# Steps of three late chains at set places between weight matmuls, GLA's odd queries side by side, and a bank of their own for the last columns

## The chip, the cores and the metric

The kernel runs on one core of one Trainium2 chip. The metric is device time in microseconds (us); a comparison takes the median of several runs. TensorE (PE) multiplies, VectorE (DVE) and ScalarE (ACT) do elementwise work and reductions, GpSimd (POOL) is hardly used, SyncE (SP) issues the transfers. PEld is TensorE's loading of stationary weights.

## The reference

One decoder layer on x of 256 tokens by 2048, all in float32:

```python
h = rms_norm(x, norm1_gain) * (1 + scale1) + shift1          # scale, shift, gate: silu(c) @ w_ada + b_ada
proj = h @ w_in                                              # 13840 columns, split among three branches
o_sb  = stick-breaking attention, 6 heads, q and k normalised
o_dil = 3 groups of 2 heads, windows (128, 1), (512, 4), (2048, 16), ALiBi, mixed by softmax of their log-denominators
o_gla = gated linear attention, 4 heads of 128 x 256, rms_norm, times silu(r)
y = g0 * (o_sb @ w_br_sb) + g1 * (o_dil @ w_br_dil) + g2 * (o_gla @ w_br_gla)      # g: sigmoid of gate columns
x = x + gate1 * (y @ w_out)
h = rms_norm(x, norm2_gain) * (1 + scale2) + shift2
x = x + gate2 * ((silu(h @ w_gate) * (h @ w_up)) @ w_ffn_out)
```

## The kernel before, in words

**Weight matmuls.** A weight block is 512 columns wide. `load_weights` (L125) brings two 128-row pieces at a time through four `raw` buffers, ScalarE rounds them to `whi` (L148) and VectorE subtracts (L149, "split") to get `wlo`. Activations are kept transposed, as a high and a low part too. `mm3` (L153) adds three products per 128-row piece k and per half t of the 256 tokens, each with 512 moving columns. `block` (L158) runs k over a block's rows, both halves inside.

**Order.** The kernel is written in a tile framework: the program is traced in order, and a builder then fixes each engine's instruction order by priority and by its own idea of when an operand is ready; on the chip each engine keeps that order. `prio()` lifts what is traced inside it ahead by 4000 places. `tc.issue_after(ins)` keeps an instruction behind another on the same engine. `tick` runs background work (the sums of `silu(c) @ w_ada` for the later modulations, on VectorE) at a set rate beside the blocks. Transposes and attention use four "misc" PSUM banks, weight blocks four "acc" banks. Scratch tiles ("scr") have three buffers.

**First chunks' h.** `first_group` (L475) forms the modulation of the first three 128-row chunks. After the last multiply-add of 16 over the conditioning (`last_mac`, L510), chunk 0's sum over partitions is a matmul with a column of ones (L301); chunks 1 and 2 are transposed (L526) and reduced by VectorE (L529), each reduction behind the low part of the chunk before. `finish_columns` (L312) adds bias and gain, `make_h` (L412) gives ScalarE's high part (L417) and VectorE's low part (L424).

**GLA.** Within a 128-token half, scores are built by levels L = 1, 2, 4, ..., 64 (`gla`, L747): keys of even segments of length L against queries of odd ones. `scatter` (L735) multiplies, for each half and each of four heads, the first 128 - L columns against the last 128 - L, and a masked copy (L742) writes what belongs to the level. A float32 matmul stands twice in the trace, since it is done in two records.

**Dilated attention.** `dilated` (L797) turns q and k (L621), computes scores (L807, L808) and their exponentials for six heads. `mixture` (L834) scales the rows of one head (L849), transposes them (L854), copies them to SBUF on ScalarE (L856) and multiplies by v (L857, L858), head by head. `dilated` is called after the first of two blocks of GLA's output gate (L941), `mixture` between the second and the third block of the branch gates (L962).

**Norm 2.** The last block of `w_out` is done half by half (L1112), and so is the first FFN block (L1141). After each half of `w_out`, `residual` (L1066) adds to x and `norm2` (L1075) forms the scale from the sum of squares (`rsqrt`, L237), and for each of four 512-column pieces scales (L1082), transposes (L1085), applies gain and shift (L1089), and splits (L1093, L1094).

**The end.** The last block of `w_ffn_out` is done half by half from row piece 30 on (L1192). `add_out` (L1172) multiplies by gate 2, adds x and stores; for the last half in two pieces of 256 columns.

Of the kernel before, what the change touches and what calls it, by code (L numbers as in the profile page):

```python
# [17 lines left out]
P = 128  # L18
# [21 lines left out]
NFF = 11  # L40
RANK = 16
# [25 lines left out]
def trunk(ctx: ExitStack, tc: tile.TileContext, I, out):  # L67
# [90 lines left out]
    def block(pss, act, src, k0, k1, c0, base=0, w=None, tiles=range(NT), go_on=False, more=False, seeded=False):  # L158
# [70 lines left out]
    def turn_vectors():  # L229
# [5 lines left out]
        nc.scalar.copy(bada, bada_ps)  # L235

# [203 lines left out]
    def proj_block(g, b, w=None, carry=False):  # L440
# [10 lines left out]
        block(pss, h_at, w_in, k0, k1, b * NB, w=w, go_on=go_on, more=carry, seeded=seeded)  # L451
# [23 lines left out]
    def first_group():  # L475
# [191 lines left out]
    def gla():  # L667
# [59 lines left out]
        sc_same = [S(f"T{2 + t}", [P, N_GLA, P]) for t in range(NT)]  # L727
        nc.vector.memset(sc_same[0], 0.0)
        nc.vector.memset(sc_same[1], 0.0)
# [5 lines left out]
        def scatter(level, lhs, rhs, L=0):  # L735

            n = P - L
            for t in range(NT):
                ps = misc_bank([P, N_GLA, P])
                for h in range(N_GLA):  # L740
                    nc.tensor.matmul(ps[:n, h, L:], at(lhs, h, t)[:, :n], at(rhs, h, t)[:, L:], start=True, stop=True)  # L741
                nc.vector.copy_predicated(  # L742
                    sc_same[t][:n, :, L:], lvl[:n, level : level + 1, L:].to_broadcast([n, N_GLA, n]), ps[:n, :, L:]
                )

        scatter(len(GLA_LEVELS), kT, qT)
        for li, L in enumerate(GLA_LEVELS + (P,)):  # L747
# [7 lines left out]
            if L < P:  # L755
                scatter(li, f, f, L)
# [17 lines left out]
        for t in range(NT):  # L774
            o = S(f"A{9 + t}", [P, N_GLA, T])
            for h2 in range(2):
                ps = misc_bank([P, 2, T])
                ss = small([P, 2])
                for i in range(2):
# [3 lines left out]
                    nc.tensor.matmul(ps[:, i, :], sc_same[t][:, h, :], vh(h, t), start=t == 0, stop=True)  # L783
# [13 lines left out]
    def dilated():  # L797
        qk_turn(dil_parts, state["mm"].ins)
# [4 lines left out]
        for h in range(N_DIL):  # L803
            cq, ck = 18 + h, 24 + h
            slope = 2.0 ** (-8.0 * (h + 1) / N_DIL)
            z = misc_bank([P, W3])
            nc.tensor.matmul(z[:, 0:P], head(cq, 0), head(ck, 0), start=True, stop=True)  # L807
            nc.tensor.matmul(z[:, P:W3].rearrange("p (t d) -> p t d", t=NT), head(cq, 1), head2(ck), start=True, stop=True)  # L808
            lg = prob[h // 2][:, h % 2, :]
            nc.vector.scalar_tensor_tensor(lg, dist[:, h // 2, :], -slope, z, op0=ALU.mult, op1=ALU.add)  # L810
            nmx = small([P, NT])
            for t, (a, b) in enumerate(spans):
                nc.vector.reduce_max(mx[:, t, h : h + 1], lg[:, a:b], axis=AX.X)
                nc.vector.tensor_scalar(nmx[:, t : t + 1], mx[:, t, h : h + 1], -1.0, None, op0=ALU.mult)
                nc.scalar.activation(
                    lg[:, a:b], lg[:, a:b], AF.Exp, bias=nmx[:, t : t + 1], accum_out=sm[:, t, h : h + 1]
                )

        lse = small([P, NT, N_DIL])
        nc.scalar.activation(lse, sm, AF.Ln)  # L820
        nc.vector.tensor_add(lse, lse, mx)
        G = lambda x, g: x[:, :, 2 * g : 2 * g + 2]
        m2 = small([P, NT, 2])
        nc.vector.tensor_max(m2, G(lse, 0), G(lse, 1))
        nc.vector.tensor_max(m2, m2, G(lse, 2))
        for g in range(3):
            nc.vector.tensor_tensor(G(lse, g), G(lse, g), m2, op=ALU.subtract)
        nc.scalar.activation(lse, lse, AF.Exp)
        den = small([P, NT, 2])
        nc.vector.tensor_add(den, G(lse, 0), G(lse, 1))  # L830
        nc.vector.tensor_add(den, den, G(lse, 2))
        return prob, sm, lse, den, spans

    def mixture(prob, sm, lse, den, spans):  # L834
# [5 lines left out]
        nc.vector.tensor_mul(coef, coef, lse)  # L840
        oT = S("OD", [P, 2, 2, T], F32R)
        for j in range(2):
            o = misc_bank([P, T])
            for g in range(3):
                h = 2 * g + j
                cv = 30 + h
                p = prob[g][:, j, :]
                for t, (a, b) in enumerate(spans):
                    nc.vector.tensor_scalar(p[:, a:b], p[:, a:b], coef[:, t, h : h + 1], None, op0=ALU.mult)  # L849

                pt = misc_bank([P, W3])
                for i in range(3):
                    with tc.issue_after(state["mm"].ins):
                        nc.tensor.transpose(pt[:, i * P : (i + 1) * P], p[:, i * P : (i + 1) * P], ident)  # L854
                pT = scr([P, W3])
                nc.scalar.copy(pT, pt)  # L856
                nc.tensor.matmul(o, head(cv, 0), pT[:, 0:T], start=g == 0, stop=False)  # L857
                nc.tensor.matmul(o[:, P:T], head(cv, 1), pT[:, T:W3], start=False, stop=g == 2)  # L858
            split_from_psum(oT[:, 0, j, :], oT[:, 1, j, :], o)
        return oT  # L860
# [69 lines left out]

    rr = []
# [298 lines left out]
```

## Time and profile before

| | us |
|---|---|
| median of 3 runs | 1616.99 (1616.95 to 1617.47) |
| profiled execution | 1617.29 |
| its span, first to last instruction | 1615.5 |
| TensorE busy | 1601.9 |
| VectorE busy | 1119.4 |
| ScalarE busy | 795.2 |
| bytes read from HBM | 392.53 MB |

The profile is of one execution; its span is a little shorter than its device time, which holds what lies before the first and after the last instruction. A timeline row reads: start, length, engine, line, operation, out<-in, partitions x elements, and how many like it were merged; in brackets the idle time of the engine before it and what ended it. A group's row gives busy time, mean ns of one, idle time before. Windows give busy time and count of each engine in a stretch, then granted clock, DMA share and GB/s. A matmul's recorded length is longer than the distance to the next one, since matmuls overlap in the array.

### The profile page before, as it was taken

Reading aid. Unit: us, or ns where it says so; the run is one execution under the profiler, and the core shown is the slowest. Engines: PE = TensorE matmul, PEld = TensorE weight load, DVE = VectorE, ACT = ScalarE, POOL = GpSimd, SP = SyncE. Lnnn points to the kernel's source line nnn. Section 1 sums busy time; section 2 is a strip of 40 time slices with the busy share of each in tenths; the row PEclk is TensorE's granted clock in tenths of the full one; section 3 lists DMA queues with packets and bytes.
Section 4 is the critical chain, followed back from the end, with each engine's and each line's share of the span. In section 5 each row is a group of like instructions: output and inputs, shape, how many; then the busy total and the mean of one; then the engine's idle time right before and its main releaser. Section 6 shows DMA issues by size and latency. Waiting matters only on the chain.

```text
span 1615.5 us, 19941 instructions
## 1 busy us (share of the span) xinstructions
PE 1601.9 (99%) x7336; PEld 1322.0 (82%) x7336; DVE 1119.4 (69%) x1301; ACT 795.2 (49%) x1116; POOL 5.3 (0%) x14
## 2 busy tenths in 40 slices
PE   8999999999999999999999999999999999999998
PEld 7888888788878888888887888888888888888887
DVE  6899995869888787878657566667645555455453
ACT  5654458765865434444446544444444444433332
POOL 1000000000000000000000000000000000000000
PEclk9999999999999999999999999999999999999999
DMA  9999997865868889898666578888666666666663
GB/s 337 355 332 323 333 301 246 268 209 171 286 209 264 305 300 312 299 313 299 229 193 199 161 250 258 267 268 272 199 187 187 189 185 191 189 205 197 205 208 106
DMA packets 194593, 395.94 MB, mean 245 GB/s; under 512 B 12914, under 2 KB 27928, under 8 KB 194496
## 3 DMA queue, kind: packets, MB, share of 16 engines
q1 hardware_dynamic: 194096, 394.60, 75.1%
q8 instruction: 57, 0.93, 0.2%
q14 instruction: 40, 0.33, 0.1%
q10 hardware_dynamic: 176, 0.07, 0.0%
q0 software_dynamic: 224, 0.01, 0.0%
HBM read 392.53 MB, written 2.10 MB: 244 GB/s over the span
## 4 chain that ended last, share of the span: by engine, by line
PE 91%; DMA 3%; DVE 3%; ACT 2%; issue 1%; SPq 0%; DVEq 0%; ACTq 0%
PE acc L156 28%; PE acc L155 28%; PE acc L154 28%; DVE wlo L149 1%; PE misc L741 1%; PE misc L1016 1%; PE acc L405 1%; DMA raw<-w_in 1%; ACT whi L148 1%; DMA raw<-w_br_gla 0%; DMA A<-x 0%; PE misc L398 0%; DVE T L259 0%; DMA T<-w_ada 0%; DMA OS<-w_ada 0%
## 5 line engine op out<-in xcount | busy, mean ns | idle before, releaser
L149 DVE TENSOR_TENSOR wlo<-raw,whi 128x1024 fp32r<-128x1024 f32 (+1 forms) x546 | 652.1, 1199 | 439.3 <-ACT whi L148 437.6
L148 ACT CAST whi<-raw 128x1024 fp32r<-128x1024 f32 (+1 forms) x546 | 562.6, 1032 | 704.9 <-PE acc L156 578.7
L154 PE MATMUL acc<-whi,H 128*128 128x512 f32 x1576 | 616.4, 391 | 1.1 <-ACT H L417 1.0
L156 PE MATMUL acc<-whi,H 128*128 128x512 f32 x1576 | 615.5, 391 | 0.4 <-DVE H L424 0.4
L155 PE MATMUL acc<-wlo,H 128*128 128x512 f32 x1576 | 615.5, 391 | 0.1
L156 PEld LDWEIGHTS acc<-whi,H 128*128 128x128 f32 x1576 | 295.8, 188 | 62.9 <-DVE H L424 1.6
L154 PEld LDWEIGHTS acc<-whi,H 128*128 128x128 f32 x1576 | 296.0, 188 | 62.2 <-ACT H L417 1.9
L155 PEld LDWEIGHTS acc<-wlo,H 128*128 128x128 f32 x1576 | 296.0, 188 | 60.5 <-DVE wlo L149 0.8
L155 PE MATMUL acc<-wlo,A 128*128 128x512 f32 x312 | 121.5, 390 | 0.5 <-DVE wlo L149 0.5
L154 PE MATMUL acc<-whi,A 128*128 128x512 f32 x312 | 121.9, 391 | 0.0
L156 PE MATMUL acc<-whi,A 128*128 128x512 f32 x280 | 109.0, 389 | 0.0
L259 DVE SCALAR_TENSOR_TENSOR ada<-AR,csil,ada 128x1024 f32<-128x1024 f32 x59 | 75.2, 1278 | 1.3 <-DMA AR<-w_ada 1.3
L155 PEld LDWEIGHTS acc<-wlo,A 128*128 128x128 f32 x312 | 58.6, 188 | 12.8 <-DVE wlo L149 0.9
L154 PEld LDWEIGHTS acc<-whi,A 128*128 128x128 f32 x312 | 58.6, 188 | 12.1
L156 PEld LDWEIGHTS acc<-whi,A 128*128 128x128 f32 x280 | 52.6, 188 | 10.9
L154 PE MATMUL acc<-whi,T 128*128 128x512 f32 x120 | 46.7, 389 | 0.0
L155 PE MATMUL acc<-wlo,T 128*128 128x512 f32 x120 | 46.7, 389 | 0.0
L156 PE MATMUL acc<-whi,T 128*128 128x512 f32 x120 | 46.7, 389 | 0.0
L156 PE MATMUL acc<-whi,OS 128*128 128x512 f32 x112 | 43.6, 389 | 0.0
L461 ACT COPY A<-acc 128x512 f32<-128x512 f32 x50 | 29.2, 586 | 18.4 <-PE acc L156 17.2
L259 DVE SCALAR_TENSOR_TENSOR ada<-OS,csil,ada 128x1024 f32<-128x1024 f32 (+2 forms) x33 | 35.6, 1077 | 1.2 <-DMA OS<-w_ada 1.0
L463 DVE TENSOR_TENSOR A<-A,acc 128x512 f32<-128x512 f32 x48 | 31.5, 682 | 2.1 <-PE acc L156 1.8
(337 smaller groups left out, 1212.3 us busy)
## 6 DMA issues: line engine op xcount, KB each, us to landing
raw<-w_in SPq DMA_DIRECT2D x205, 512.0 KB, 4.9
raw<-w_ffn_in SPq DMA_DIRECT2D x176, 512.0 KB, 3.8
raw<-w_ffn_out SPq DMA_DIRECT2D x88, 512.0 KB, 4.5
AR<-w_ada SPq DMA_DIRECT2D x79, 512.0 KB, 4.9
raw<-w_out SPq DMA_DIRECT2D x32, 512.0 KB, 4.0
KC<-w_ada SPq DMA_DIRECT2D x30, 512.0 KB, 5.7
OS<-w_ada SPq DMA_DIRECT2D x16, 512.0 KB, 6.5
raw<-w_br_gla SPq DMA_DIRECT2D x16, 512.0 KB, 6.4
```

Source lines behind the costliest of these rows:

```text
L148: state["cast"] = nc.scalar.copy(hi[:, :n, :], raw[:, :n, :])
L149: state["split"] = nc.vector.tensor_tensor(lo[:, :n, :], raw[:, :n, :], hi[:, :n, :].bitcast(F32), op=ALU.subtract)
L154: nc.tensor.matmul(ps, lh, rh, start=start, stop=False, skip_group_check=seeded)
L155: nc.tensor.matmul(ps, lh, rl, start=False, stop=False, skip_group_check=seeded)
L156: state["mm"] = nc.tensor.matmul(ps, ll, rh, start=False, stop=stop, skip_group_check=seeded)
L259: nc.vector.scalar_tensor_tensor(acc, raw, c, acc, op0=ALU.mult, op1=ALU.add)
L405: state["warm"] = nc.tensor.matmul(ps, ones_r, wide, start=True, stop=True)
L461: nc.scalar.copy(A[b][:, t, :], pss[t])
L463: nc.vector.tensor_add(A[b][:, t, :], A[b][:, t, :], pss[t])
L741: nc.tensor.matmul(ps[:n, h, L:], at(lhs, h, t)[:, :n], at(rhs, h, t)[:, L:], start=True, stop=True)
L1016: nc.tensor.transpose(ps[:, i, :], src[:, i * P : (i + 1) * P], ident)
```

## The change

Five edits. (1) In `first_group` all three last multiply-adds come first, and chunk 1 is summed by the matmul with ones, as chunk 0. (2) In GLA, a level's matmuls move only the queries of odd segments, 64 columns, side by side, for both halves into one bank, and one masked copy writes all. The zeroed score tile of both halves is one tile. (3) Dilated attention is cut into steps that `block` calls ahead of row piece k, behind the matmul before it and with priority: two turns and two score steps in the second block of GLA's output gate, and, after all rows have been scaled, turns and products in the second block of the branch gates. (4) Norm 2 scales all four pieces into one 2048-column tile right after its half; its 16 transposes and what follows are a step at k = 10 of the other half and k = 11 of the first FFN block's first half. The scale is applied as two factors, and two small multiplies fall away. (5) In the last half, the last four row pieces are multiplied for the first 256 columns, then for the last 256 into another bank; the first 256 columns and the part sums of the last are added to x while those run.

```diff
+N2_AT = (10, 11)
...
 def block(..., steps=None):
+            if steps and k - k0 in steps:
+                with tc.issue_after(state["mm"].ins), prio():
+                    steps[k - k0]()
...
+    def rsqrt_parts(ss, inv_n, shape):
+        v = small(shape)
+        nc.vector.tensor_scalar(v, ss, inv_n, EPS, op0=ALU.mult, op1=ALU.add)
+        y = small(shape)
+        nc.scalar.activation(y, v, AF.Ln)
+        nc.scalar.activation(y, y, AF.Exp, scale=-0.5)
+        z = small(shape)
+        nc.vector.scalar_tensor_tensor(z, y, y, v, op0=ALU.mult, op1=ALU.mult)
+        nc.vector.tensor_scalar(z, z, -0.5, 1.5, op0=ALU.mult, op1=ALU.add)
+        return y, z
...
-        last_mac(0)
-        last_mac(1)
+        for q in range(n):
+            last_mac(q)
...
-            if q == 0:
+            if q < 2:
                 sums = misc_bank([P, 2])
...
-            if q == 0:
-                with tc.issue_after(state["finish"].ins):
-                    last_mac(2)
...
-        def scatter(level, lhs, rhs, L=0):
-            n = P - L
-            for t in range(NT):
-                ps = misc_bank([P, N_GLA, P])
-                for h in range(N_GLA):
-                    nc.tensor.matmul(ps[:n, h, L:], at(lhs, h, t)[:, :n], at(rhs, h, t)[:, L:], start=True, stop=True)
-                nc.vector.copy_predicated(
-                    sc_same[t][:n, :, L:], lvl[:n, level : level + 1, L:].to_broadcast([n, N_GLA, n]), ps[:n, :, L:]
-                )
+        def scatter(level, f, L):
+            n, ns = P - L, P // (2 * L)
+            odd = lambda x: x.rearrange("p (s two l) -> p s two l", two=2, l=L)[:, :, 1, :]
+            ps = misc_bank([P, NT * N_GLA, P // 2])
+            for t in range(NT):
+                for h in range(N_GLA):
+                    nc.tensor.matmul(
+                        ps[:n, t * N_GLA + h, :].rearrange("p (s l) -> p s l", l=L), at(f, h, t)[:, :n], odd(at(f, h, t)),
+                        start=True, stop=True,
+                    )
+            dst = sc_same.rearrange("p b (s two l) -> p b s two l", two=2, l=L)[:n, :, :, 1, :]
+            mask = lvl[:n, level, :].rearrange("p (s two l) -> p s two l", two=2, l=L)[:, :, 1, :]
+            nc.vector.copy_predicated(
+                dst, mask.unsqueeze(1).to_broadcast([n, NT * N_GLA, ns, L]),
+                ps[:n].rearrange("p b (s l) -> p b s l", l=L)
+            )
...
+    def mixture_rows(prob, sm, lse, den, spans):
...
+        for h in range(N_DIL):
+            p = prob[h // 2][:, h % 2, :]
+            for t, (a, b) in enumerate(spans):
+                nc.vector.tensor_scalar(p[:, a:b], p[:, a:b], coef[:, t, h : h + 1], None, op0=ALU.mult)
+    def mixture(prob):
+        oT = S("OD", [P, 2, 2, T], F32R)
+        def turn(j):
+            out = []
+            for g in range(3):
+                pt = misc_bank([P, W3])
+                for i in range(3):
+                    nc.tensor.transpose(pt[:, i * P : (i + 1) * P], prob[g][:, j, i * P : (i + 1) * P], ident)
+                pT = scr([P, W3])
+                nc.scalar.copy(pT, pt)
+                out.append(pT)
+            return out
...
+        def first():
+            turned.append(turn(0))
+        def second():
+            products(0, turned[0])
+            turned.append(turn(1))
+        return oT, {4: first, 7: second, 10: lambda: products(1, turned[1])}
...
+    dil_scores, dil_weights = dilated()
+    dil_steps = {
+        2: lambda: qk_turn(dil_parts[:2]),
+        5: lambda: qk_turn(dil_parts[2:]),
+        8: lambda: dil_scores(0, 3),
+        11: lambda: dil_scores(3, 6),
+    }
...
-        block(pss, h_at, w_in, 0, KC, (13 + j) * NB)
+        block(pss, h_at, w_in, 0, KC, (13 + j) * NB, steps=dil_steps if j else None)
...
-        if j == 0:
-            groups = dilated()
...
-    for br in range(2):
-        gate_block(0, br)
+    with prio():
+        groups = dil_weights()
+        mixture_rows(*groups)
+    gate_block(0, 0)
     ring["tags"] = ("AR0", "AR1", "KC", "KD")
-    od = mixture(*groups)
+    od, turns = mixture(groups[0])
+    gate_block(0, 1, turns)
     gate_block(0, 2)
...
-    def norm2(t):
+    def norm2_rows(t):
...
+        r, r2 = rsqrt_parts(ss, 1.0 / D, [P, 1])
+        xs = S("ada", [P, D])
+        for j in range(KC // 4):
+            nc.vector.tensor_scalar(
+                xs[:, j * NB : (j + 1) * NB], x2[j][:, t, :], r, r2, op0=ALU.mult, op1=ALU.mult
+            )
+        return xs
+    def norm2_turn(t, xs):
...
         for j in range(KC // 4):
-            xs = scr([P, NB])
-            nc.vector.tensor_scalar(xs, x2[j][:, t, :], r, None, op0=ALU.mult)
             ps = misc_bank([P, 4, P])
             for i in range(4):
-                nc.tensor.transpose(ps[:, i, :], xs[:, i * P : (i + 1) * P], ident)
+                k = 4 * j + i
+                nc.tensor.transpose(ps[:, i, :], xs[:, k * P : (k + 1) * P], ident)
+            banks.append(ps)
+        for j, ps in enumerate(banks):
...
-        block({t: ps}, y_at, None, 0, KC, 0, w=w, tiles=(t,))
+        block({t: ps}, y_at, None, 0, KC, 0, w=w, tiles=(t,), steps={N2_AT[0]: lambda: norm2_turn(0, xs)} if t else None)
         with prio():
             residual(3, t, ps)
-            norm2(t)
+            xs = norm2_rows(t)
...
-                block(pg, h2_at, None, 0, KC, 0, w=w, tiles=(t,))
+                block(pg, h2_at, None, 0, KC, 0, w=w, tiles=(t,), steps=None if t else {N2_AT[1]: lambda: norm2_turn(1, xs)})
...
+            block(pss, act_at, None, CUT, KF - LASTK, 0, w=w, tiles=(1,), go_on=True, more=True)
+            side = acc_bank()
+            for cols, ps in ((slice(0, NB - LASTC), pss[1][:, : NB - LASTC]), (slice(NB - LASTC, NB), side[:, :LASTC])):
+                for k in range(KF - LASTK, KF):
+                    wh, wl = w[k - CUT]
+                    h, l = act_at(k, 1)
+                    mm3(ps, h, l, wh[:, cols], wl[:, cols], k == KF - LASTK and cols.start > 0, k == KF - 1)
+                if cols.start == 0:
+                    add_out(n, 1, pss[1], end=NB - LASTC)
+                    add_out(n, 1, pss[1], NB - LASTC, store=False)
+            add_out(n, 1, side, NB - LASTC, base=NB - LASTC)
```

More of the change, by code (lines that the diff above doesn't have):

```diff
@@ L156, in mm3, with block @@
         state["mm"] = nc.tensor.matmul(ps, ll, rh, start=False, stop=stop, skip_group_check=seeded)
-    def block(pss, act, src, k0, k1, c0, base=0, w=None, tiles=range(NT), go_on=False, more=False, seeded=False):
+    def block(pss, act, src, k0, k1, c0, base=0, w=None, tiles=range(NT), go_on=False, more=False, seeded=False,
+              steps=None):
         if w is None:
@@ L450, in proj_block @@
             go_on = True
-        block(pss, h_at, w_in, k0, k1, b * NB, w=w, go_on=go_on, more=carry, seeded=seeded)
+        block(pss, h_at, w_in, k0, k1, b * NB, w=w, go_on=go_on, more=carry, seeded=seeded, steps=steps)
         if carry:
@@ L802, in dilated @@
         spans = ((0, P), (P, W3))
[L803 to L816, printed above, removed]
-                )
@@ L830, in dilated, with scores @@
[L830 to L834, printed above, removed]
+        def scores(h0, h1):
+            for h in range(h0, h1):
+                cq, ck = 18 + h, 24 + h
+                slope = 2.0 ** (-8.0 * (h + 1) / N_DIL)
+                z = misc_bank([P, W3])
+                nc.tensor.matmul(z[:, 0:P], head(cq, 0), head(ck, 0), start=True, stop=True)
+                nc.tensor.matmul(z[:, P:W3].rearrange("p (t d) -> p t d", t=NT), head(cq, 1), head2(ck), start=True, stop=True)
+                lg = prob[h // 2][:, h % 2, :]
+                nc.vector.scalar_tensor_tensor(lg, dist[:, h // 2, :], -slope, z, op0=ALU.mult, op1=ALU.add)
+                nmx = small([P, NT])
+                for t, (a, b) in enumerate(spans):
+                    nc.vector.reduce_max(mx[:, t, h : h + 1], lg[:, a:b], axis=AX.X)
+                nc.vector.tensor_scalar(nmx, mx[:, :, h], -1.0, None, op0=ALU.mult)
+                for t, (a, b) in enumerate(spans):
+                    nc.scalar.activation(
+                        lg[:, a:b], lg[:, a:b], AF.Exp, bias=nmx[:, t : t + 1], accum_out=sm[:, t, h : h + 1]
+                    )
@@ L835, in mixture @@
+        return scores, weights
+    def mixture_rows(prob, sm, lse, den, spans):
         G = lambda x, g: x[:, :, 2 * g : 2 * g + 2]
```

89 lines of the change are left out of this document (45 added, 44 removed).

## The prediction

> **What bounds the kernel now.** I read the page first (busy shares and the chain), then TensorE's busy time in a stretch that holds nothing but weight matmuls, then TensorE's waits by releaser, then the timeline of the five places that the change touches.
>
> ```profile
> PE 1601.9 (99%) x7336; PEld 1322.0 (82%) x7336; DVE 1119.4 (69%) x1301; ACT 795.2 (49%) x1116; POOL 5.3 (0%) x14
> ...
> PE 91%; DMA 3%; DVE 3%; ACT 2%; issue 1%; SPq 0%; DVEq 0%; ACTq 0%
> ...
> L154 PE MATMUL acc<-whi,H 128*128 128x512 f32 x1576 | 616.4, 391 | 1.1 <-ACT H L417 1.0
> ```
>
> TensorE is busy 99% of the span, and 91% of the chain that ended last is TensorE. A matmul's recorded length (391 ns) is modelled, so I ask how far apart matmuls start. In a stretch of the down projection without any other TensorE work:
>
> ```profile
> 1400.00:1590.00 190.00, 190.00 (x840) 1.00 0.64 202
> ```
>
> 840 matmuls of 512 columns in 190.0 us are 0.226 us each, at clock 1.00. The change takes away no weight matmul. So it can win only what TensorE stands still, or a cheaper small matmul. TensorE's waits that the profile names:
>
> ```profile
> PE acc L154 <- ACT H L417: 1.0, 2, 0.7
> PE misc L854 <- DVE T L849: 0.8, 1, 0.8
> ...
> PE misc L1085 <- DVE scr L1082: 0.6, 2, 0.4
> ```
>
> (Columns: us in total, times, longest.) The first belongs to the first chunks' h, the second to the dilated mixture, the last to norm 2. These few tenths are understated: a recorded matmul lasts 0.39 us where the next could start after 0.226, so each wait hides about 0.17 more. The whole stake is a few microseconds in 1617. About 0.2% (3.2 us) is what a measurement of this kernel can tell from no change.
>
> **The change part by part.** Profiled execution: 1617.29 us, its span 1615.5.
>
> *First chunks' h.* VectorE and TensorE rows of the timeline, then two windows (columns ending in clock, DMA share, GB/s):
>
> ```profile
> 30.98 0.48 DVE L259 SCALAR_TENSOR_TENSOR ada<-A,csil,ada 128x256 f32<-128x256 f32 x1
> 32.23 0.42 DVE L529 TENSOR_REDUCE tiny<-misc 128x2 f32<-128x256 f32 x1
> 33.07 0.40 PE L156 MATMUL acc<-whi,H 128*128 128x512 f32 x1
> 33.79 0.51 PE L154 MATMUL acc<-whi,H 128*128 128x512 f32 x1 [0.32 <-ACT H L417]
> 34.44 0.68 DVE L149 TENSOR_TENSOR wlo<-raw,whi 128x512 fp32r<-128x512 f32 x1
> 35.06 0.40 PE L156 MATMUL acc<-whi,H 128*128 128x512 f32 x1
> 36.15 0.50 PE L154 MATMUL acc<-whi,H 128*128 128x512 f32 x1 [0.69 <-ACT H L417]
> ...
> 35.00:40.00 5.00, 4.18 (x17) 2.72 (x17) 4.71 (x10) 4.39 (x7) 0.00 (x0) 1.00 0.90 292
> 40.00:80.00 40.00, 40.00 (x178) 33.12 (x177) 34.42 (x35) 24.97 (x39) 0.00 (x0) 1.00 0.99 353
> ```
>
> TensorE loses 33.79 - 33.07 - 0.226 = 0.49 before chunk 1 and 36.15 - 35.06 - 0.226 = 0.86 before chunk 2. The change takes the 0.48 multiply-add (30.98) from between the chunks and, for chunk 1, the 0.42 reduction with its place behind chunk 0's low part; two more one-column matmuls do the sum on a TensorE that stands there anyway. Chunk 1's wait should go. Chunk 2 keeps its reduction and the 0.68 split at 34.44 ahead of it, so it comes forward only by the 0.85 that VectorE saves (0.42 and 0.48, less 0.05 for the reordered start), and waits longer behind a chunk 1 that ended earlier. Locally that is 0.85. What is late next is the transfers: DMA engines are 0.99 busy from 40 to 80 us, so TensorE can be ahead only by what they make up in the gap at 35 to 40 (0.10 of 5 us = 0.5). I take **-0.5**, ends 0 and -0.85.
>
> *GLA's odd queries side by side.* Rows of the groups by shape (busy us, mean ns, idle before): a one-column matmul, two levels, and VectorE's masked copy:
>
> ```profile
> L301 PE MATMUL misc<-ones_r,ada 128*128 128x1 f32 x4 | 0.6, 248 | 0.0
> ...
> L741 PE MATMUL misc<-T 128*127 128x127 f32 x16 | 1.9, 274 | 0.0
> ...
> L741 PE MATMUL misc<-T 128*64 128x64 f32 x16 | 1.1, 225 | 0.0
> ...
> L742 DVE COPY_PREDICATED T<-KC,misc 127x508 f32<-127x508 uint8 x2 | 1.5, 732 | 0.0
> ```
>
> Level 1 takes (1.9 - 0.27)/15 = 0.109 us a matmul, with 127 weight columns and 127 moving ones. The change makes the moving ones 64 and leaves the weights' number. The L301 group moves a single column against 128 weight columns and still steps by (0.6 - 0.25)/3 = 0.12. So weight columns set the pace, and TensorE saves **0**. If moving columns set it, each of six levels would fall from at most 1.9 to the 1.1 of level 64, at most 4.8 and, with the levels between, about 4.3; that is a rival below. VectorE saves one masked copy in two per level, at most 7 x 0.73 = 5.1. I price this at nothing: TensorE fills the GLA chain with projection matmuls, and no named wait is on L742's results. End above zero: 0.3, if a wait moves.
>
> The Trainium skill ("TensorE: Matmul & The Clock Gate", section "The mechanism" of its part on packing small matmuls) states that a weight load overlaps a running matmul only when their row groups differ. By it, load and move would add, and fewer moving columns would save the about 4.3. The trace disagrees: 0.12 with 1 moving column is no less than 0.109 with 127.
>
> *Dilated attention and mixture.*
>
> ```profile
> 463.84 0.39 PE L154 MATMUL acc<-whi,H 128*128 128x512 f32 x1
> 464.60 0.75 DVE L849 TENSOR_SCALAR T<-T,dcoef 128x128 f32<-128x128 f32 x3
> 465.04 0.30 PE L854 MATMUL misc<-ident,T 128*128 128x128 f32 x1 [0.81 <-DVE T L849]
> 465.09 0.48 PE L155 MATMUL acc<-wlo,H 128*128 128x512 f32 x1
> ...
> 474.20 0.48 PE L155 MATMUL acc<-wlo,H 128*128 128x512 f32 x1
> 475.02 0.70 PE L857 MATMUL misc<-scr,A 128*128 128x256 f32 x2 [0.34 <-ACT scr L856]
> ```
>
> 465.04 - 463.84 - 0.226 = 0.97 lost on the first scaled row, 475.02 - 474.20 - 0.226 = 0.59 on a copy by ScalarE: 1.56. The code writes three transposes in a row under one ordering edge, yet a weight matmul stands between the first and the second (465.09). So an ordering edge is a floor, and the builder fills by its own idea of what is ready; a "set place" is a floor too. The new code scales all rows before any transpose and turns all three groups of one output before their products, so a product no longer waits for one fresh copy, and there are fewer points at which TensorE can be early. The same matmuls remain. I take the 1.56 as gone and about 0.2 as left at new points: **-1.4**, ends -2.1 (with half a microsecond of small waits between 436 and 477 that I see only in start distances) and +0.5. The steps issue no DMAs. The loads that take the distance table's buffer come one block earlier behind the scores, on SP's queue, with weight loads behind them; at 0.70 to 0.75 DMA share there that is slack.
>
> *Norm 2.* A window (TensorE alone: busy, count, clock, DMA), then VectorE:
>
> ```profile
> 866.00:897.00 31.00, 30.20 (x144) 1.00 0.44 137
> ...
> 863.61 0.69 DVE L1070 TENSOR_TENSOR scr<-T,acc 128x512 f32<-128x512 f32 x1 [2.34 <-PE acc L156]
> ...
> 871.55 0.16 DVE L248 TENSOR_TENSOR tiny<-tiny,tiny 128x1 f32<-128x1 f32 x1
> 871.74 0.48 DVE L1082 TENSOR_SCALAR scr<-A,tiny 128x512 f32<-128x512 f32 x1
> 872.17 1.23 DVE L149 TENSOR_TENSOR KD<-raw,A 128x1024 fp32r<-128x1024 f32 x1
> 873.31 0.48 DVE L1082 TENSOR_SCALAR scr<-A,tiny 128x512 f32<-128x512 f32 x1
> ...
> 877.47 0.49 DVE L1082 TENSOR_SCALAR scr<-A,tiny 128x512 f32<-128x512 f32 x1
> ```
>
> 144 records touch the window: 32 transposes at 0.109 (3.5) and 112 matmuls at 0.226 (25.3), 28.8 of 31.0; with two that began before it, 2.2 to 2.6 are lost. They come from four scaled rows per half that arrive singly (871.74 to 877.47), held by three scratch buffers and by 1.23 us splits between them. After: one buffer for all four, so they can follow each other at about 0.48, the pace of four transposes (0.44); the chain to the scale loses two small instructions. Half 0's rows were due 871.74 - 863.61 = 8.1 us after its last matmul; the floor at k = 10 lies 30 x 0.226 = 6.8 us after it. The chain saves 0.3, or 1.5 if one split less stands in it, so the transposes start near the floor with a wait of some tenths. ScalarE then has the last six k, 18 x 0.226 = 4.1 us, before the first FFN matmul wants its part. I leave 0.5 per half: 2.5 - 1.0 = **-1.5**, ends -2.5 and +0.5.
>
> *Last columns.*
>
> ```profile
> 652.75 0.28 PE L895 MATMUL misc<-T,ones_r 128*128 128x256 f32 x1
> 652.87 0.28 PE L896 MATMUL misc<-T,ones_r 128*128 128x256 f32 x1
> ...
> 1610.30 0.39 PE L156 MATMUL acc<-H,H 128*128 128x512 f32 x1
> 1610.72 0.75 DVE L1178 TENSOR_TENSOR scr<-ada,acc 128x256 f32<-128x256 f32 x2 [8.11 <-PE acc L156]
> 1611.39 0.75 DVE L1180 TENSOR_TENSOR A<-A,scr 128x256 f32<-128x256 f32 x2
> 1611.84 0.83 SPq L1181 DMA_DIRECT2D out<-A  x2
> ```
>
> After the last matmul stand two multiplies and two adds, 1610.72 to 1612.14. With an own bank one multiply and one add are left, 0.75 as for any two in a row: 0.67 less. 24 matmuls of 256 columns at 0.12 replace 12 of 0.226: 2.88 against 2.71, 0.17 more. The other four VectorE instructions (1.42 as now) lie beside the last 12 matmuls (1.44). **-0.5**, ends -0.6 and -0.2. The store after it stays.
>
> Sum: -0.5 + 0 - 1.4 - 1.5 - 0.5 = -3.9, so 1617.3 - 3.9 = 1613.4 for a profiled execution. It lay 0.3 above the median of 1616.99, so I forecast **1613.1**.
>
> **The rivals.**
>
> *The floors bind nothing.* The builder puts the steps where it thinks them ready, as now, and TensorE waits as long at fewer points. Only the end and half of the start stay, with half of one other part: -0.5 - 0.25 - 0.75 = -1.5, **1615.5**. For it: the waits now come from misjudged readiness, and the change adds no knowledge of VectorE's splits.
>
> *Moving columns set GLA's pace*: 4.3 more, **1608.8**. Against it: the L301 group.
>
> *Slower: norm 2's transposes stand as one run of 16 ahead of the matmuls.* Today a late row delays four transposes, and matmuls stand between. If VectorE still puts a split between rows, the fourth is scaled at 872.2 + 3 x (1.23 + 0.48) = 877.3, while TensorE could have finished the run at 863.6 + 6.8 + 16 x 0.109 = 872.1: 5.2 and 0.4 for its own transposes, 5.6 lost; half 1, with its floor one k later and fewer splits left, about half of that, 2.8. That is 8.4 against the 2.5 lost now, and with -2.4 from the rest +3.5: **1620.5**. It decides from 2.5 + 2.4 = 4.9 us of waits at the two places together. Against it: rows in a buffer of their own have nothing to wait for and stand ahead of later weights by priority.
>
> **How the numbers follow.** Forecast 0.58 (own range 1611.3 to 1615.0), floors that bind nothing 0.22, GLA's moving columns 0.07, norm 2's run 0.13. The line for faster is 1616.99 - 3.23 = 1613.8. Two thirds of the forecast's chance lie below it (0.39), with GLA's 0.07 0.46; the rest and the second case are within: 0.41; slower 0.13. The range takes the ends of all parts: -0.85 + 0 - 2.1 - 2.5 - 0.6 = -6.0 and 0 + 0.3 + 0.5 + 0.5 - 0.2 = +1.1, from 1617.0: 1610.9 to 1618.1. Outside it are the last two cases, 0.20.
>
> **What would show it.** Start: no wait before chunk 1, one below 0.9 before chunk 2, and a longer one near 91 us if the transfers take it back. GLA: groups of 16 at level 1 still near 1.9, nine masked copies in place of sixteen. Mixture: no wait of 0.5 or more on the scaled rows. Norm 2: four rows within 2 us, and under 1.2 lost from 866 to 897. End: one multiply and one add after the last matmul. The forecast is wrong if runs of 16 transposes show waits of microseconds, or if weight splits move and TensorE waits at places that the change doesn't touch.

## The result: 1619.32 us, slower by 0.15%

| | before | after |
|---|---|---|
| median | 1616.99 us (1615.5 to 1619.01, 20 runs) | 1619.32 us (1616.87 to 1621.62, 20 runs) |
| ratio | | 1.0015, 95% interval 1.0008 to 1.0021 |
| profiled execution, its span | 1617.29, 1615.5 | 1620.85, 1618.9 |

The forecast was 1613.1, its range ended at 1618.1: the result lies 1.2 above the range, and on the other side of no change, though by less than the 0.2% that the prediction set as its line. The profiled execution of after is 1.5 above its own median; a stretch at half clock that lies in it is shown in the last section.

The page of after (line numbers are after's: `mm3` is now L155 to L157, the cast to `whi` L149, the split L150):

```profile
PE 1603.4 (99%) x7350; PEld 1324.5 (82%) x7350; DVE 1117.2 (69%) x1284; ACT 797.7 (49%) x1118; POOL 5.3 (0%) x14
...
PE 93%; DMA 2%; ACT 2%; DVE 2%; issue 1%; SPq 0%; ACTq 0%; DVEq 0%
```

VectorE has 17 instructions and 2.2 us less, ScalarE two more. TensorE is still the bound. Its waits by releaser in after:

```profile
PE misc L638 <- DVE A L626: 2.3, 1, 2.3
PE acc L156 <- DVE wlo L150: 1.6, 3, 0.8
PE misc L896 <- DVE T L884: 1.5, 1, 1.5
...
PE acc L155 <- ACT H L1170: 0.7, 1, 0.7
```

The two largest single ones are new, and both lie in dilated attention: the first turn of the normalised q and k (L638 behind the scaling L626), and the first scaled row of the mixture (L896 behind L884). The 1.6 on split weights (L150) is three waits, of which those at 84.36 and 582.68 us are the large ones. Norm 2's largest is 0.7.

**Where the time went, by stage.** From the trace I take each TensorE record's distance to the next, subtract the usual distance of its kind (0.2267 us for 512 moving columns, 0.109 for 128x128, the median of the kind otherwise), and sum what is left:

| stage, us | before | after |
|---|---|---|
| 30 to 93, first chunks' h | 4.0 | 3.6 |
| 432 to 480, dilated attention | 2.9 | **6.4** |
| 860 to 897, norm 2 | 2.6 | 2.4 |

(300 to 330 and 560 to 600 us also differ, 1.8 against 0.9 and 0.8 against 1.8; among the profiles below they swing from 0.9 to 2.4 and from 0.0 to 1.8 between kernels that have the same code there.)

**Dilated attention.** ScalarE's rows in the timeline of before:

```profile
431.97 0.21 ACT L242 ACTIVATE tiny<-tiny 128x24 f32<-128x24 f32 x1
432.22 0.22 ACT L243 ACTIVATE tiny<-tiny 128x24 f32<-128x24 f32 x1
...
435.29 1.28 ACT L968 ACT_TABLE_LOAD   x1
436.58 1.06 ACT L968 ACTIVATE A<-A 128x1024 f32<-128x1024 f32 x1
```

L242 and L243 are the Ln and Exp of the factor that normalises the dilated q and k. L968 is the sigmoid of a branch gate, which is used only when the branches' outputs are multiplied by it, after the whole of attention; to use it, ScalarE first loads another table. The same stretch in after:

```profile
435.31 1.28 ACT L1035 ACT_TABLE_LOAD   x1
436.61 1.06 ACT L1035 ACTIVATE A<-A 128x1024 f32<-128x1024 f32 x1
438.62 1.28 ACT L262 ACT_TABLE_LOAD   x1
...
442.07 1.28 ACT L263 ACT_TABLE_LOAD   x1
443.36 0.22 ACT L263 ACTIVATE tiny<-tiny 128x24 f32<-128x24 f32 x1
```

The sigmoid is at the same time, but now **ahead of** the Ln (its load at 438.62) and the Exp (443.36). Each of them has a table load of its own, and weight casts stand between: the Exp comes at 443.36 in place of 432.22, 11.1 us later. On VectorE, then on TensorE:

```profile
446.56 1.36 DVE L626 TENSOR_TENSOR A<-A,tiny 128x256 f32<-128x256 f32 x3
```

```profile
447.04 0.77 PE L638 MATMUL misc<-ident,A 128*128 128x128 f32 x4 [2.30 <-DVE A L626]
```

TensorE keeps the builder's order, so it stands for the turn at 447.04. At the softmax of the weights it happens again: L858 is the Ln, L866 the Exp, and a second gate's sigmoid slipped between them: three loads within about 6 us.

```profile
467.19 1.28 ACT L858 ACT_TABLE_LOAD   x1
...
469.66 1.28 ACT L1035 ACT_TABLE_LOAD   x1
470.95 1.06 ACT L1035 ACTIVATE A<-A 128x1024 f32<-128x1024 f32 x1
472.03 1.28 ACT L866 ACT_TABLE_LOAD   x1
```

```profile
476.22 0.30 PE L896 MATMUL misc<-ident,T 128*128 128x128 f32 x1 [1.51 <-DVE T L884]
```

**Theory**: the loss is the gates' sigmoids, put on ScalarE ahead of and between the small functions of the dilated chain. **Rivals**: the set places themselves make TensorE wait ("steps"), or the loss lies elsewhere. That leaves open which of the five edits moved the sigmoid. In the programs that the builder writes for each edit alone, only the **GLA** edit, not the dilated one, turns ScalarE's order; the traces of e3 and of e5 to e8 below show the same.

### The profile page after: what moved, and what is told of

It reads as the page before. It is cut to its first block, busy times and chain, and to the rows that moved or that the text cites. A ratio compares the mean times of both kernels' runs of the same rounds, so it can differ in the third digit from the quotient of the medians.

```text
span 1618.9 us, 19946 instructions
## 1 busy us (share of the span) xinstructions
PE 1603.4 (99%) x7350; PEld 1324.5 (82%) x7350; DVE 1117.2 (69%) x1284; ACT 797.7 (49%) x1118; POOL 5.3 (0%) x14
## 4 chain that ended last, share of the span: by engine, by line
PE 93%; DMA 2%; ACT 2%; DVE 2%; issue 1%; SPq 0%; ACTq 0%; DVEq 0%
PE acc L157 29%; PE acc L156 29%; PE acc L155 29%; DMA raw<-w_br_gla 1%; PE misc L1083 1%; PE acc L425 1%; PE misc L769 1%; DVE wlo L150 1%; ACT whi L149 1%; DMA A<-x 0%; PE misc L418 0%; DMA raw<-w_in 0%; PE misc L329 0%; ACT scr L1166 0%; DMA raw<-w_ffn_in 0%
## 5 line engine op out<-in xcount | busy, mean ns | idle before, releaser
L150 DVE TENSOR_TENSOR wlo<-raw,whi 128x1024 fp32r<-128x1024 f32 (+1 forms) x546 | 652.1, 1198 | 442.2 <-ACT whi L149 440.2
L149 ACT CAST whi<-raw 128x1024 fp32r<-128x1024 f32 (+1 forms) x546 | 561.9, 1032 | 698.8 <-PE acc L157 574.8
L155 PE MATMUL acc<-whi,H 128*128 128x512 f32 x1576 | 616.5, 392 | 1.5 <-ACT H L437 0.8
L157 PE MATMUL acc<-whi,H 128*128 128x512 f32 x1576 | 615.8, 391 | 0.4 <-DVE H L444 0.4
L157 PEld LDWEIGHTS acc<-whi,H 128*128 128x128 f32 x1576 | 295.9, 188 | 63.2 <-DVE H L444 1.6
L155 PEld LDWEIGHTS acc<-whi,H 128*128 128x128 f32 x1576 | 296.2, 188 | 62.5 <-ACT H L437 1.3
L155 PE MATMUL acc<-whi,A 128*128 128x512 f32 x312 | 122.0, 391 | 0.4 <-ACT whi L149 0.4
L157 PE MATMUL acc<-whi,A 128*128 128x512 f32 x280 | 109.0, 389 | 0.0
L155 PEld LDWEIGHTS acc<-whi,A 128*128 128x128 f32 x312 | 58.6, 188 | 12.8 <-ACT whi L149 0.8
L157 PEld LDWEIGHTS acc<-whi,A 128*128 128x128 f32 x280 | 52.6, 188 | 10.9
L155 PE MATMUL acc<-whi,T 128*128 128x512 f32 x120 | 46.7, 389 | 0.0
L157 PE MATMUL acc<-whi,T 128*128 128x512 f32 x120 | 46.7, 389 | 0.0
L157 PE MATMUL acc<-whi,OS 128*128 128x512 f32 x112 | 43.6, 389 | 0.0
```

The lines of the kernel that those rows point to most:

```text
L149: state["cast"] = nc.scalar.copy(hi[:, :n, :], raw[:, :n, :])
L150: state["split"] = nc.vector.tensor_tensor(lo[:, :n, :], raw[:, :n, :], hi[:, :n, :].bitcast(F32), op=ALU.subtract)
L155: nc.tensor.matmul(ps, lh, rh, start=start, stop=False, skip_group_check=seeded)
L157: state["mm"] = nc.tensor.matmul(ps, ll, rh, start=False, stop=stop, skip_group_check=seeded)
```

## The experiments

Line numbers in the rows are those of the kernel named. Each comparison has the kernel before run beside it.

| kernel | median (runs) | before beside it | 95% interval of the ratio | lost 432 to 480 | table loads 430 to 490 |
|---|---|---|---|---|---|
| before | | | | 2.9 | 5 |
| after | 1619.32 (20) | 1616.99 | 1.0008 to 1.0021 | 6.4 | 7 |
| e1 after, sigmoids held | 1615.97 (11) | 1616.93 | 0.9986 to 1.0003 | 3.4 | 1 |
| e2 before, sigmoids held | 1616.24 (11) | 1616.93 | 0.9987 to 1.0005 | 2.2 | 1 |
| e3 before + GLA edit | 1620.94 (9) | 1616.93 | 1.0015 to 1.0034 | 5.2 | 7 |
| e4 after - GLA edit | 1614.49 (11) | 1616.93 | 0.9973 to 0.9991 | 1.3 | 5 |
| e5 before + start | 1617.03 (11) | 1617.29 | 0.9989 to 1.0007 | 2.9 | 5 |
| e6 before + dilated edit | 1615.17 (11) | 1617.29 | 0.9980 to 0.9998 | 1.3 | 5 |
| e7 before + norm 2 | 1617.21 (11) | 1617.29 | 0.9990 to 1.0007 | 2.9 | 5 |
| e8 before + end | 1616.74 (11) | 1617.29 | 0.9988 to 1.0006 | 2.9 | 5 |
| e9 after, held behind the Exp | 1616.09 (11) | 1617.35 | 0.9985 to 1.0003 | 2.6 | 5 |
| e10 after, held, norm early | 1614.18 (11) | 1617.35 | 0.9971 to 0.9989 | 1.0 | 1 |
| e11 after - GLA edit, held | 1615.08 (11) | 1617.35 | 0.9975 to 0.9993 | 2.2 | 1 |
| e12 before + an extra sigmoid | 1619.26 (11) | 1617.35 | 1.0001 to 1.0019 | 4.2 | 8 |

**e1: after, with the sigmoids held.**

```diff
 def turn(j): ...
-                nc.scalar.copy(pT, pt)
+                state["mix_end"] = nc.scalar.copy(pT, pt)
...
     for br in range(3):
-        nc.scalar.activation(gates[0, br], gates[0, br], AF.Sigmoid)
+        with tc.issue_after(state["mix_end"].ins):
+            nc.scalar.activation(gates[0, br], gates[0, br], AF.Sigmoid)
```

> After with one edit: the three sigmoids of the branch gates (L1035) may be issued on ScalarE only behind the mixture's last copy (L898). Theory 'misplaced sigmoid': the changed kernel loses because a sigmoid stands ahead of the dilated q and k's Ln and Exp and another between the softmax's Ln and Exp, each with table loads of 1.28 us; it stands 2.46 us at 447 us, about 1.3 more in a half-clock stretch, and 1.68 at 476. Held back, six table loads go, and with them these waits: 3.8 to 5 us off the changed kernel's 1619.3, so 1614.3 to 1615.5, 1.5 to 2.7 below the kernel before. Rival 'steps': the fixed places themselves make TensorE wait for VectorE's chain: still 1618.5 to 1619.5, as the loads lie beside other work. Rival 'elsewhere' (transfers near 580 us, norm 2): the two waits go but the time stays within 1 us of 1619.3.

1615.97, 3.35 below after: the theory holds, "steps" as the whole cause doesn't. It is 0.5 above the range that I gave, so something is left. ScalarE in e1, and TensorE's waits in the same stretch:

```profile
437.32 0.21 ACT L262 ACTIVATE tiny<-tiny 128x24 f32<-128x24 f32 x1
437.56 0.22 ACT L263 ACTIVATE tiny<-tiny 128x24 f32<-128x24 f32 x1
...
472.16 1.28 ACT L1036 ACT_TABLE_LOAD   x1
```

```profile
439.93 0.78 PE L638 MATMUL misc<-ident,A 128*128 128x128 f32 x4 [0.59 <-DVE A L626]
444.43 0.66 PE L638 MATMUL misc<-ident,A 128*128 128x128 f32 x4 [0.91 <-DVE A L626]
```

One load is left of seven. But the Exp still comes at 437.56, 5.3 us after that of before. This residue is taken up in e10.

**e2: before, with the same edit** (its copy is that of `mixture`).

```diff
-        nc.scalar.activation(gates[0, br], gates[0, br], AF.Sigmoid)
+        with tc.issue_after(state["mix_end"].ins):
+            nc.scalar.activation(gates[0, br], gates[0, br], AF.Sigmoid)
```

> Before with the same edit alone (sigmoids of the branch gates behind the mixture's last copy). In before the sigmoid stands behind the Ln and Exp of the dilated q and k but loads tables at 435.3, 444.1, 454.3, 461.0 and 464.5 us. Theory 'misplaced sigmoid': four loads go, the scaled rows come up to 5 us earlier, and the 0.97 and 0.59 us that TensorE stands at 465 and 475 us shrink: 1615.5 to 1616.5 against 1617.0. Rival 'steps': the loads do not matter, 1617.0.

1616.24: on the theory's side by its place, but the interval holds no change. The stage lost 2.2 in place of 2.9.

**e3: before with the GLA edit alone** (`scatter`, `sc_same` and their uses as in the change).

```diff
-                scatter(li, f, f, L)
+                scatter(li, f, L)
```

> Before with the GLA edit alone (odd queries side by side, one masked copy per level); dilated attention as before. In its program the builder already puts the sigmoid ahead of the dilated q and k's Ln and Exp, as in the changed kernel, with ten table loads in place of eight. Theory 'misplaced sigmoid, by way of the GLA edit': slower than before by 2 to 4.5 us, 1619.0 to 1621.5, with the waits near 447 us and later on dilated attention. Rival 'steps': GLA alone costs nothing, 1616.7 to 1617.3. Rival 'moving columns': 1612.7.

1620.94, 4.0 above the kernel before, with dilated attention as it always was. The waits of e3 and its loads:

```profile
PE misc L621 <- DVE A L609: 2.5, 1, 2.5
PE misc L871 <- DVE T L866: 1.6, 1, 1.6
```

```profile
435.08 1.28 ACT L985 ACT_TABLE_LOAD   x1
...
438.39 1.28 ACT L242 ACT_TABLE_LOAD   x1
...
442.03 1.28 ACT L243 ACT_TABLE_LOAD   x1
```

They are after's picture: L985 is the sigmoid, L242 and L243 the Ln and Exp. The GLA edit alone turns the order, and costs more than the whole change. Not all of the 4.0 is in the profile: the profiled execution of e3 took 1619.38, 2.1 above that of before, and 2.3 more is lost from 432 to 480 us. Where the median's other 1.9 lies is not shown; the last section has a candidate.

**e4: after without the GLA edit.** `scatter`, `sc_same` and their uses are those of before.

```diff
-                scatter(li, f, L)
+                scatter(li, f, f, L)
```

> After with the GLA edit undone, all else changed. The sigmoid stands behind the Ln and Exp again. Theory 'misplaced sigmoid, by way of the GLA edit': 1614.0 to 1615.5, so faster than before by 1.5 to 3. Rival 'steps': 1618.5 to 1619.5, as after. Rival 'transfers took it all back': 1616.5 to 1617.5.

1614.49, faster than the kernel before. No wait is left on L638's operands there, and the order is that of before:

```profile
432.01 0.22 ACT L263 ACTIVATE tiny<-tiny 128x24 f32<-128x24 f32 x1
...
435.07 1.28 ACT L1018 ACT_TABLE_LOAD   x1
```

**e5 to e8: each other edit alone on before**, the lines of the change; one of each is shown.

```diff
-            if q == 0:
+            if q < 2:
                 sums = misc_bank([P, 2])
```

> Before with the first edit alone (chunk 1 summed by the matmul with ones, the last multiply-adds first). The prediction's term: -0.5 us (1616.4). Theory 'transfers take it back', from the trace of after (1.6 less lost from 30 to 40 us, 1.1 more from 40 to 93): 0, 1616.7 to 1617.2, with TensorE's place at 93 us as in before within 0.2.

```diff
-        block(pss, h_at, w_in, 0, KC, (13 + j) * NB)
+        block(pss, h_at, w_in, 0, KC, (13 + j) * NB, steps=dil_steps if j else None)
```

> Before with the dilated edit alone (steps at set places, rows scaled ahead, turns and products apart). ScalarE's program keeps the sigmoid behind the Ln and Exp of the dilated q and k. The prediction's term: -1.4 us. Theory 'misplaced sigmoid, by way of the GLA edit': the term holds where GLA is as before, 1615.0 to 1616.0, and 432 to 480 us loses 1.2 to 1.6 in place of 2.9. Rival 'steps': the set places cost what they gain, 1616.7 to 1617.3, or more.

```diff
-            norm2(t)
+            xs = norm2_rows(t)
```

> Before with the norm 2 edit alone. The prediction's term: -1.5 us (1615.5). From after's trace (2.4 lost from 860 to 897 us in place of 2.6) and that of the kernel without the GLA edit (2.0): -0.2 to -0.6, 1616.3 to 1616.8. The prediction's slower rival: +6, 1623.

```diff
+    LASTK, LASTC = 4, NB // 2
```

> Before with the last edit alone (own bank for the last 256 columns). The prediction's term: -0.5 us, 1616.2 to 1616.7, with one multiply and one add after the last matmul, about 0.7 less from the last matmul to the last store's issue, and 0.2 more of matmuls. Rival: the store's own time hides it, 1617.0.

The times of e5 and e6 are where their theories put them. E7's 1617.21 lies above the 1616.3 to 1616.8 read from the traces, a miss, and e8's 1616.74 just above its range. Start -0.3, dilated -2.1, norm 2 -0.1, end -0.5 against the kernel before beside them; only the dilated one's interval lies off 1. With e3's +4.0 they sum to +1.0, where the whole change measured +2.3; five intervals of about 1.5 us to either side allow that.

**e9: after, sigmoids held only behind the Exp of the dilated q and k.** `qk_exp` is that Exp.

```diff
     for br in range(3):
-        nc.scalar.activation(gates[0, br], gates[0, br], AF.Sigmoid)
+        with tc.issue_after(qk_exp.ins):
+            nc.scalar.activation(gates[0, br], gates[0, br], AF.Sigmoid)
```

> After with the branch gates' sigmoids held only behind the Exp of the dilated q and k, not behind the mixture. ScalarE's program then has eight table loads, in the places of before, but the squares of q and k still end late. If the loads ahead of q and k's factor are what costs, 432 to 480 us loses 3 to 4 us as with the full hold (3.4), and the time is 1615.5 to 1616.5. If the late squares alone cost it, 5 to 6.4 us stay lost there: 1618 to 1619.5. Rival 'steps': 1619.3.

1616.09, 3.2 below after, and 432 to 480 us loses 2.6, less than I had said: with five loads, those of before. So a hold behind that Exp brings nearly all of e1's gain. But the sigmoid between the softmax's Ln and Exp went back by itself, so e9 undoes both places and does not price them apart.

**e10: after, held, and the dilated norm early.**

```diff
-    qk_norm(dil_parts)
+    with prio():
+        qk_norm(dil_parts)
```

> After with the full hold of the sigmoids and, besides, the norm of the dilated q and k traced with priority. With the hold alone TensorE still stands 0.75 and 1.08 us on the normalised q and k at 440 and 444 us, since their last square ends at 435.3 and not at 430.7. Theory 'GLA edit shifts ScalarE's order': with the squares early as well, 432 to 480 us loses 0.6 to 1.5 (as without the GLA edit, 1.3), so 1613.5 to 1614.8. Rival: the GLA edit has a cost of its own elsewhere, or the early squares push GLA's own norms or weight casts back: 1616 or more.

1614.18, and 1.0 lost in the stage. With the sigmoids and the squares both put back, the kernel is as fast with the GLA edit as e4 is without it (1614.49). The early norm was not tried without the GLA edit, so a small cost of its own is not ruled out. This is the fastest median of the study: ratio to before 0.9980 (0.9971 to 0.9989), 5.1 below after.

**e11: after without the GLA edit, sigmoids held**: the edits of e4 and e1 together.

```diff
-                scatter(li, f, L)
+                scatter(li, f, f, L)
...
+        with tc.issue_after(state["mix_end"].ins):
```

> After with the GLA edit undone and the sigmoids held behind the mixture. Without the hold it was 1614.5 and lost 1.3 us from 432 to 480. The four table loads go; what is left to win there is 0 to 0.7: 1613.7 to 1614.6.

A miss: 1615.08, not below e4's 1614.49, and the stage lost 2.2 in place of e4's 1.3, 0.76 of it on a turn at 440.3. The Ln and Exp of q and k stand at 431.92 and 432.17 there, as in e4, so the four loads that went lay beside other work, and taking them away won nothing. What makes the turn at 440.3 wait is not shown.

**e12: before with one more sigmoid.** It touches neither GLA nor the order of the squares.

```diff
 def rsqrt(ss, inv_n, shape, first=None): ...
+        if first is not None:
+            nc.scalar.activation(y, v, first)
         nc.scalar.activation(y, v, AF.Ln)
...
-    qk_norm(dil_parts)
+    qk_norm(dil_parts, AF.Sigmoid)
```

> Before with one more instruction on ScalarE: a sigmoid of 24 columns (0.2 us) just ahead of the Ln of the dilated q and k, its result overwritten by the Ln, so two table loads stand in that chain (2.6 us by the 1.28 of one). GLA, squares and all else as before. If table loads in this chain reach TensorE, 432 to 480 us loses 4 to 5.5 in place of 2.9: 1618 to 1619.5. If they lie beside other work: 1616.8 to 1617.3.

1619.26, 1.9 above the kernel before (the interval only just clears 1), and 4.2 lost in the stage. It brought three loads to the chain, not the two that I expected: at 432.74 for the sigmoid, 436.18 for the Ln and 438.66 for the Exp. A 0.2 us instruction of another table set, put in that chain, is enough to make the kernel slower.

## Why the prediction was wrong

**The failed step is GLA's.** The prediction said of the fewer masked copies: "I price this at nothing: TensorE fills the GLA chain with projection matmuls, and no named wait is on L742's results. End above zero: 0.3, if a wait moves." That the work itself is cheap was right. TensorE's and VectorE's groups in after:

```profile
L769 PE MATMUL misc<-T 128*127 128x64 f32 x16 | 1.9, 269 | 0.0
...
L769 PE MATMUL misc<-T 128*64 128x64 f32 x16 | 1.1, 225 | 0.0
```

```profile
L775 DVE COPY_PREDICATED T<-KC,misc 127x512 f32<-127x512 uint8 x1 | 1.3, 1327 | 0.2 <-PE misc L769 0.2
...
L775 DVE COPY_PREDICATED T<-KC,misc 64x512 f32<-64x512 uint8 x1 | 0.7, 740 | 0.0
```

Level 1 takes 1.9 us with 64 moving columns as with 127: the rival "moving columns set GLA's pace" is dead, weight columns set it. But the edit cost 4.0 us (e3), and beside the other edits 4.8 (after less e4), through instructions that it doesn't name. First, GLA's chain itself comes later. The last level in before, then in e3:

```profile
395.02 1.15 PE L741 MATMUL misc<-T 128*64 128x64 f32 x16
```

```profile
399.51 1.15 PE L752 MATMUL misc<-T 128*64 128x64 f32 x16
```

TensorE doesn't stand for it (345 to 420 us loses 2.1 in both), so this costs nothing there. But behind it ScalarE's fixed order changed. The last square of the dilated q and k, in before, then in after:

```profile
430.51 0.30 ACT L601 ACTIVATE scr<-A 128x128 f32<-128x128 f32 x1
```

```profile
434.90 0.30 ACT L618 ACTIVATE scr<-A 128x128 f32<-128x128 f32 x1
```

The squares start 1.5 us later (420.79 in place of 419.26), and a further weight cast and two copies of a gate's block (L1018) stand among them. Besides, a sigmoid moved ahead of their Ln. By e9 the sigmoids' places are worth 3.2 us of after's time; by e10 against e1, which differ in nothing else, the late squares 1.8. What in the builder's reckoning turned the order was not tried.

The prediction had the rule in its hands (each engine keeps the order that the builder wrote by its own idea of readiness) and used it for TensorE's transposes only. It had no row of ScalarE's table loads, though before's timeline shows five between 435 and 465 us.

**Dilated attention, -1.4: right where the order held.** 432 to 480 us loses 1.3 in e4 and e6 against 2.9, so -1.6; e6's median is -2.1. "Floors bind nothing" falls with that here. In after the term turned into +3.5.

**First chunks' h, -0.5: nothing measurable.** TensorE in before, then in after:

```profile
90.92 0.73 PE L156 MATMUL acc<-whi,H 128*128 128x512 f32 x2 [0.37 <-DVE H L424]
```

```profile
84.36 0.50 PE L156 MATMUL acc<-wlo,H 128*128 128x512 f32 x1 [0.67 <-DVE wlo L150]
...
90.94 0.73 PE L157 MATMUL acc<-whi,H 128*128 128x512 f32 x2 [0.40 <-DVE H L444]
```

The wait before chunk 1 went. So did that before chunk 2, which the prediction had growing: its first matmul starts at 35.05 with no wait named, in before at 36.15 behind 0.69. From 30 to 40 us after loses 1.6 in place of 3.2. A new wait for weights at 84.36 gives much of it back (40 to 93 us loses 2.0 in place of 0.9), and both kernels stand at 90.9 for the low part of a later chunk. The prediction's end 0 was the answer: a gain ahead of a place where both kernels wait for the same thing ends there.

**Norm 2, -1.5: half of the size, and the floor didn't bind.** The seven profiles without the edit lose 2.6 to 3.2 from 860 to 897 us (mean 3.0), the seven with it 1.8 to 2.6 (mean 2.2): -0.8. E7's median shows none of it (-0.1, and the interval holds no change). After's rows, VectorE, then TensorE:

```profile
875.62 1.91 DVE L1148 TENSOR_SCALAR ada<-A,tiny,tiny 128x512 f32<-128x512 f32 x4
```

```profile
876.30 2.00 PE L1160 MATMUL misc<-ident,ada 128*128 128x128 f32 x16 [0.17 <-DVE ada L1148]
...
881.47 0.50 PE L155 MATMUL acc<-whi,H 128*128 128x512 f32 x1 [0.65 <-ACT H L1170]
```

Four rows in 1.91 us and a wait of tenths, as forecast. But the transposes do not start near the floor: k = 10 asks for 30 matmuls of half 1 ahead of them, and 37 stand there, in all seven profiles with the edit. As in the rival "floors bind nothing", the builder set the step later than its floor. So ScalarE had 11 matmuls before the first FFN matmul, 2.5 us, in place of the 18 and 4.1 us of the prediction. ScalarE's rows:

```profile
878.11 1.05 ACT L149 CAST A<-raw 128x1024 fp32r<-128x1024 f32 x1 [1.94 <-DMA raw<-w_ffn_in]
...
880.79 0.63 ACT L1170 CAST H<-scr 128x512 fp32r<-128x512 f32 x1
```

A weight cast that waited for its transfer until 878.11 stands ahead of the gains. The first high part ends at 881.42, which is where TensorE waited: 5.2 us after the first transpose. The slower rival's run of 16 did come, without its late rows: it lasts 2.00 us.

**Last columns, -0.5: right by the rows.** VectorE in e8:

```profile
1601.21 0.69 DVE L1177 TENSOR_TENSOR scr<-ada,acc 128x512 f32<-128x512 f32 x1 [2.60 <-PE acc L156]
...
1611.33 0.42 DVE L1179 TENSOR_TENSOR A<-A,scr 128x256 f32<-128x256 f32 x1
```

The last add ends 10.54 us after half 0's multiply starts; in before it was 10.94 (1601.20 to 1612.14). So -0.40. E8's median is -0.5, though its interval holds no change.

Without the GLA edit the other four make 1614.49 (e4), 1.4 above the forecast and inside its own range, but also only 1.0 below the rival that the floors bind nothing. By the rows, the dilated term was right, the end nearly, and norm 2 and the start were set too large.

## What to carry to other kernels

Where a scheduler writes the engines' orders, an edit's price is not only its own instructions: after pricing them, list what stands next in each in-order queue behind the edited place, and what could change places there. On ScalarE look first for functions of other table sets near a chain that TensorE waits for, and hold what isn't needed soon behind that chain. As the first chunks' h showed, a gain in front of a place where both kernels wait for the same thing ends there.

## What the runs showed of the hardware

**A table load takes 1.28 us, and a sigmoid costs more than its own.** The kernel itself loads, by name, a set of functions that holds both Ln and Exp: `preload_act_table_set("natural_log_exp_and_others")`, in before at 2.16 us (L189) and again at 774.85 (L1054). Until the first sigmoid Ln and Exp run from it. In e1, with the sigmoids held, neither needs a load (437.32 and 437.56 above). In after, behind a sigmoid, a load stands ahead of the Ln (438.62) and another ahead of the Exp (442.07), with nothing but a weight cast between the two functions. Before has the same at 454.29 and 461.03, with three weight casts between. The Trainium skill ("ScalarE: Activation LUTs", section "Table sets: the hidden batching unit") says that Ln followed by Exp takes one load, since one set has both. That fits e1, where the named set serves both; it doesn't fit the pairs of loads in after and before, where no set had been loaded by name again. Loading that set by name behind the sigmoid would be another way to spare loads; it was not tried.

**A stand of 2.3 us was followed by half a clock.** Windows of after (the third-last column is the granted clock):

```profile
446.00:448.00 2.00, 0.96 (x6) 0.70 (x7) 1.90 (x7) 0.15 (x1) 0.00 (x0) 1.00 0.64 170
448.00:449.00 1.00, 1.00 (x7) 0.96 (x5) 1.00 (x2) 0.54 (x1) 0.00 (x0) 0.54 0.77 297
449.00:451.00 2.00, 2.00 (x6) 1.55 (x6) 2.00 (x5) 0.00 (x0) 0.00 (x0) 0.50 0.36 62
451.00:452.00 1.00, 1.00 (x7) 0.79 (x6) 1.00 (x3) 0.27 (x1) 0.00 (x0) 0.75 0.97 371
```

By these clocks the halved stretch is 0.92 + 2.00 + 0.50 = 3.4 us long. It lies in the stage in which after loses 1.2 more than e3, whose profile has a like stand (2.48 us) and full clock there. Of after's 20 runs 13 show a mean clock of 0.998 or 0.999 and average 1619.9, the other 7 show 1.000 and average 1618.4. Of e3's nine, five show the lower clock and average 1621.7, the other four 1619.6. That the slower ones had such a stretch is possible but not shown: only one of after's was profiled, and the profiles of e2, e6, e7 and e12 also show a mean of 0.999 with full clock from 10 to 1610 us. The Trainium skill ("TensorE: Matmul & The Clock Gate", section "What's actually happening") gives half rate after an idle window of about 3.4 us that runs on its own. The halved stretch is as long as that window; the stand ahead of it was shorter, 2.3 us.

**A masked copy of 512 elements per row has two prices**: 1.33 and 1.31 us where it writes single columns or pairs (levels 1 and 2), 0.70 to 0.74 from runs of four on. So nine copies of 7.6 us in all replaced sixteen of 10.0.
